# Output projection and second MLP matrix of a two-layer trunk: products of 512 columns instead of 256, and the weight block in the outer loop

## The chip, the core and the metric

One core of one Trainium2 chip runs the whole program in one launch. The metric is the device time of an execution in microseconds (us), lower is better. The kernel before takes 1643.44 us (median of 3 runs, 1642.19 to 1646.79).

## What is computed

Two layers over 256 latent tokens and 256 context tokens of width 1024, all in float32. In the last layer the context only gives keys and values, so what lies behind the mixer runs over 512 tokens in the first layer and over 256 in the last. The part that matters here:

```python
def merge_out(gates, ys, wb, bb, wo):
    ...                                   # merged: (tokens, 1024)
    return merged @ wo                    # wo: (1024, 1024)

def sq_relu_ffn(h, w1, w2):
    a = jax.nn.relu(h @ w1)               # (tokens, 4096)
    return (a * a) @ w2                   # w2: (4096, 1024)

x = layer_norm(DEEPNORM_ALPHA * x + g1 * y, ln_g[l, 0], ln_b[l, 0])
x = layer_norm(DEEPNORM_ALPHA * x + g2 * sq_relu_ffn(x * (1.0 + sc2) + sh2, w_ff1[l], w_ff2[l]),
               ln_g[l, 1], ln_b[l, 1])
```

## The kernel before, in words

**Arithmetic.** Every float32 operand is split into a high part (rounded to the matmul's float32 format) and a low part (what is left). A product is three matmuls: high times high, high times low, low times high (`mm3`, L424). The program's names show it: `whi` and `wlo` are the two parts of a weight unit, `mg` the merged branches (in pairs of tiles, high and low), `a` the squared activations of the MLP.

**Weight units.** All weights come in units of 128 partitions x 1024 values (512 KB). For each unit SyncE issues a transfer into one of three `raw` buffers (`w_load`), ScalarE copies it to one of three `whi` buffers (`w_hi`), VectorE subtracts to one of three `wlo` buffers and frees the raw one (`w_lo`). A unit's `whi` and `wlo` come free when TensorE has read them for the last time. Units come in the order of `weight_order` (L614), the order in which the matmuls use them.

**The two products of this case.** In the output projection (`out_proj`, tile name `wo`) and the second MLP matrix (`ff2`, tile name `f`) the tokens are the stationary operand: one matmul has 128 tokens as weights and streams 256 columns of a weight unit. A unit holds 512 rows (4 blocks k of 128) of 256 output columns. Outer loop: four column blocks nb of 256; both units of the block are fetched (`weights`, L599); inner loop: the tiles of 128 tokens; per tile 8 k times 3 matmuls into one PSUM bank, then the next tile. So in a token tile the 24 matmuls run over all 8 k before the next tile begins, and the two units of a block are held until the last tile has used them. The MLP's 4096 rows come in four quarters (qd 0 to 3) of 1024, with stretches of the first MLP matrix (`ff1`, tile name `mm`) between them; the quarters are summed in `yacc` on VectorE. In layer 0, `out_proj` and the last quarter run over two pairs of token tiles (s = 0, 1), the other quarters over all four; in layer 1 there is one pair.

**What follows a product.** `residual` (L1413) multiplies the PSUM result by the gate row, adds the scaled input, and takes the norm's statistics (BN_STATS), each on VectorE over 256 columns; in a last quarter the input was added ahead (`ffn_residual`). `norm_tile` waits for the four statistics of a token tile and normalises it (`r` is such a tile; `st` its statistics); TensorE transposes it (`uT`), ScalarE and VectorE make the next product's operand `u`.

**Order of the work.** A list scheduler at build time (`Sched.run`) replays costs and priorities and writes one fixed order per engine; at run time each engine goes through its own list in order and waits on semaphores. The modulation sums of layer 1 (`sums`, from transfers named `araw`) are woven into layer 0 on VectorE and ScalarE; `araw` has two buffers. In the last layer four of a stage's eight units serve each token tile in turn (`blocks`, L607: the first two column blocks for both tiles, then the other two for tile 0 alone, then for tile 1); two of those units are held in other buffers (`wh`, `wl`).

Of the kernel before, what the change touches and what calls it, by code (L numbers as in the profile page):

```python
# [54 lines left out]
def unit_table():  # L55

    names = []
    for m in range(76):
        if not (M_DV <= m < M_DV + 4 or M_NV <= m < M_NV + 4):
            names.append(("in", m))  # L60
    for br in ("dv", "nv"):
        names += [(br, s, h) for s in range(2) for h in range(2)]
    names += [("br", i, mp) for i in range(4) for mp in range(4)]
    names += [("wo", nb, h) for nb in range(4) for h in range(2)]
    names += [("f1", m) for m in range(32)]
    names += [("f2", qd, nb, h) for qd in range(4) for nb in range(4) for h in range(2)]
    return {n: i for i, n in enumerate(names)}
# [237 lines left out]
class Kernel(Sched):  # L305
# [126 lines left out]
    def gemm(self, out, pairs, cost):  # L432
# [3 lines left out]
        for i in range(0, n, step):  # L436
            calls, r = [], []
            for j in range(i, min(n, i + step)):
                a, b = pairs[j]
                calls += self.mm3(out, a, b, j == 0, j == n - 1)  # L440
                r += [a[0], a[1], b[0], b[1]]
            yield self.mm(calls, [out], r, (cost + 2) * len(calls))

# [145 lines left out]
    def weight(self, l, *name):  # L589
# [6 lines left out]
        kn = 128 if name[0] in ("in", "f1") else 256  # L596
        return Weight(w, kn)

    def weights(self, l, name):  # L599
        w = []  # L600
        for h in range(2):
            x = yield from self.weight(l, *name, h)
            w.append(x)
        return w

    @staticmethod
    def blocks(l):  # L607

        both = (0, 1)
        if l < DEPTH - 1:  # L610
            return [(nb, both) for nb in range(4)]
        return [(0, both), (1, both), (2, (0,)), (3, (0,)), (2, (1,)), (3, (1,))]

    def weight_order(self):  # L614
        o = []
        for l in range(DEPTH):
# [37 lines left out]
            for s in range(S):  # L654
                for nb in range(4):
                    a("wo", nb, 0)
                    a("wo", nb, 1)
            f1 = lambda m0, m1: [a("f1", m) for m in range(m0, m1)]
            f2 = lambda qd: [a("f2", qd, nb, h) for nb in range(4) for h in range(2)]
# [730 lines left out]
    def normalise(self, r, stv, gb=None):  # L1390

        nc = self.nc
        st4 = stv[:, 0:24].re("p (c n) -> p c n", n=6)
# [19 lines left out]
    def residual(self, l, j, s, t, cols, ps, r, x, gB, stv, part):  # L1413

        nc = self.nc
        if part is None:
            yield self.tt(r, ps, gB, ALU.mult)
            self.release(ps)
            yield self.stt(r, x, ALPHA, r, ALU.mult, ALU.add)
        else:  # L1420
            f = yield self.s("tmp", F32, "yf")
            yield self.tt(f[:, 0:256], ps, gB, ALU.mult)
            self.release(ps)
            yield self.wait("pre", l, t, cols)
            yield self.tt(r, f[:, 0:256], r, ALU.add)
            self.release(f)
        o = stv[:, cols * 6:cols * 6 + 6]
        yield self.dve(335, lambda: nc.vector.bn_stats(out=o.ap, in_=r.ap), [o], [r])
        self.signal("res", l, j, t, cols)
# [20 lines left out]
    def norm_tile(self, l, j, t, r, stv):  # L1450
# [5 lines left out]
        for nb in range(4):  # L1456
            yield self.wait("res", l, j, t, nb)
# [3 lines left out]
        yield from self.normalise(r, stv, gb)  # L1461
# [23 lines left out]
    def out_proj(self, l, s, merged):  # L1485
# [14 lines left out]
        ws = {}  # L1500
        for nb, which in self.blocks(l):
            if nb not in ws:
                ws[nb] = yield from self.weights(l, ("wo", nb))
            w = ws[nb]
            c = slice((nb % 2) * 256, (nb % 2) * 256 + 256)
            for i in which:
                ps = yield self.alloc("ps", "main", name="wo")
                tk = slice(s * 256 + i * 128, s * 256 + i * 128 + 128)
                yield from self.gemm(ps[:, 0:256], [(self.cut(merged[k], (slice(None), tk)), w[k // 4](k % 4))
                                                    for k in range(KD)], 107)  # L1510
                self.spawn(self.residual(l, 0, s, 2 * s + i, nb, ps[:, 0:256], rs[i][nb // 2][:, c],
                                         xs[i][nb // 2][:, c], gB[nb // 2][:, c], sts[i], None), 2)
            if which[-1] == 1:
                for x in w:
                    self.release(*x.views())
        self.spawn(self.free_rows(("gB", l, 0, s), [("res", l, 0, 2 * s + i, nb) for i in range(2) for nb in range(4)]), 50)
# [53 lines left out]
    def ff2_evac(self, l, qd, t, nb, ps, y):  # L1570
# [5 lines left out]
        if qd == 2:  # L1576
            self.spawn(self.ffn_residual(l, t, nb, y), 55)

    def ffn_residual(self, l, t, nb, y):
# [3 lines left out]
        c = slice((nb % 2) * 256, (nb % 2) * 256 + 256)  # L1583
        yield self.tt(y, y, gB[nb // 2][:, c], ALU.mult)
        yield self.stt(y, x[nb // 2][:, c], ALPHA, y, ALU.mult, ALU.add)
        self.signal("pre", l, t, nb)

    def ff2(self, l, qd, tiles, last):
# [14 lines left out]
        ws = {}  # L1603
        for nb, which in self.blocks(l) if last else [(nb, range(len(tiles))) for nb in range(4)]:
            if nb not in ws:
                ws[nb] = yield from self.weights(l, ("f2", qd, nb))
            w = ws[nb]
            c = slice((nb % 2) * 256, (nb % 2) * 256 + 256)
            for t in [tiles[i] for i in which]:
                ps = yield self.alloc("ps", "main", name="f2")  # L1610
                tk = slice(t * 128, t * 128 + 128)
                yield from self.gemm(ps[:, 0:256], [(self.cut(a2[k], (slice(None), tk)), w[k // 4](k % 4))
                                                    for k in range(8)], 107)
# [259 lines left out]
```

## Time and profile before

| | |
|---|---|
| median of 3 runs | 1643.44 us (1642.19 to 1646.79) |
| the profiled execution | 1644.06 us |
| its span, first to last instruction | 1642.3 us |
| granted TensorE clock, mean | 0.99 |
| TensorE busy | 1604.0 us, 98% of the span |
| VectorE busy | 1298.5 us, 79% |
| ScalarE busy | 884.6 us, 54% |
| DMA, mean | 155 GB/s |

A row of the profile gives an engine, its line, the operation, the output and inputs by the program's names, the shape and the count; times in a row are us unless marked ns. All matmuls are issued on L423, transposes on L449. `PE` is TensorE, `PEld` its loading of the stationary operand, `DVE` VectorE, `ACT` ScalarE, `SP` SyncE (which issues all transfers). The duration that is printed for a matmul is a model of its end; the distance between starts is measured.

### The profile page before, as it was taken

The page shows a single profiled execution, that of the slowest core. Times are in us where ns is not written, and L with a number is a line of the kernel's source. Part 1 is how long each engine was busy: PE and PEld are TensorE (multiplying, and loading weights), DVE is VectorE, ACT ScalarE, POOL GpSimd, SP SyncE. Part 2 cuts the span into 40 slices and gives each one's busy share as a digit, 9 for nine tenths or more (in the row PEclk, how much of TensorE's full clock was granted, in tenths as well). Part 3 has the DMA queues.
Part 4 walks back from the last instruction along what each step waited for, and adds up shares of the span by engine and source line. Part 5 has one row for each costly group of instructions (what it writes and reads, how often), then busy time and mean ns, then how long its engine had stood idle before and what let it go on. Part 6 is the DMA issues. An engine that isn't in the chain of part 4 may idle for free.

```text
span 1642.3 us, 26846 instructions
## 1 busy us (share of the span) xinstructions
PE 1604.0 (98%) x10568; PEld 1451.5 (88%) x10568; DVE 1298.5 (79%) x2285; ACT 884.6 (54%) x1444; POOL 11.0 (1%) x51
## 2 busy tenths in 40 slices
PE   7999999999999999999999999998999999989997
PEld 4888888887888889889898889998999999989997
DVE  3899999699999448875877866999999796774566
ACT  3475484556655344642524324665677675466553
POOL 0000000000000000000000000000000000000000
PEclk9999999999999999999999999999999999999999
DMA  9322322553552345455656634634353445636563
GB/s 356 114 81 77 97 74 90 186 189 126 176 172 95 109 148 182 158 192 161 208 175 207 219 98 134 192 115 141 114 163 125 146 133 185 226 129 183 187 218 119
DMA packets 81299, 254.55 MB, mean 155 GB/s; under 512 B 9092, under 2 KB 14980, under 8 KB 81172
## 3 DMA queue, kind: packets, MB, share of 16 engines
q1 hardware_dynamic: 81172, 252.84, 47.5%
q8 instruction: 82, 1.34, 0.3%
q14 instruction: 45, 0.37, 0.1%
HBM read 250.67 MB, written 2.13 MB: 154 GB/s over the span
## 4 chain that ended last, share of the span: by engine, by line
PE 89%; DMA 5%; DVE 4%; ACT 2%; issue 1%; SPq 0%; POOLq 0%; POOL 0%; DVEq 0%; ACTq 0%
PE mm L423 50%; PE f L423 13%; PE br L423 8%; PE v L423 5%; PE wo L423 4%; PE o L423 2%; DMA araw<-in_w_ada 2%; PE S L423 2%; PE PT L449 1%; DVE wlo L376 1%; DMA a<-in_w_ada 1%; DVE sums L403 1%; ACT whi L369 1%; PE ada L423 1%; SPq L414 0%
## 5 line engine op out<-in xcount | busy, mean ns | idle before, releaser
L423 PE MATMUL mm<-u,whi 128*128 128x512 f32 (+1 forms) x3168 | 791.8, 341 | 2.4 <-ACT u L369 1.6
L369 ACT ACTIVATE whi<-raw 128x1024 fp32r<-128x1024 f32 x335 | 354.4, 1059 | 481.5 <-PE mm L423 236.9
L423 PEld LDWEIGHTS mm<-u,whi 128*128 128x128 f32 x3168 | 548.3, 192 | 67.1 <-ACT u L369 2.5
L376 DVE TENSOR_TENSOR wlo<-raw,whi 128x1024 fp32r<-128x1024 f32 x335 | 408.7, 1222 | 198.4 <-ACT whi L369 195.2
L423 PE MATMUL mm<-u,wlo 128*128 128x512 f32 (+1 forms) x1584 | 536.3, 339 | 0.8 <-DVE wlo L376 0.8
L423 PEld LDWEIGHTS mm<-u,wlo 128*128 128x128 f32 x1584 | 303.5, 192 | 32.6 <-DVE wlo L376 1.0
L423 PE MATMUL f<-whi,a 128*128 128x256 f32 x1504 | 276.6, 285 | 0.5 <-ACT a L369 0.2
L423 PEld LDWEIGHTS f<-whi,a 128*128 128x128 f32 x1504 | 237.0, 193 | 3.6 <-issue 2.5
L423 PE MATMUL f<-wlo,a 128*128 128x256 f32 x752 | 213.8, 284 | 2.6 <-DVE wlo L376 2.6
L403 DVE SCALAR_TENSOR_TENSOR sums<-araw,cs,sums 128x512 f32<-128x512 f32 x280 | 194.8, 744 | 25.3 <-DMA araw<-in_w_ada 25.0
L423 PEld LDWEIGHTS f<-wlo,a 128*128 128x128 f32 x752 | 145.0, 193 | 3.4 <-DVE wlo L376 3.2
L403 DVE SCALAR_TENSOR_TENSOR conf<-glu,sm,conf 128x512 f32<-128x512 f32 (+1 forms) x240 | 137.9, 612 | 1.0
L423 PE MATMUL v<-whi,u 128*128 128x256 f32 x512 | 96.7, 283 | 0.3 <-DVE pt L376 0.3
L423 PEld LDWEIGHTS v<-whi,u 128*128 128x128 f32 x512 | 81.6, 191 | 1.5 <-PE S L423 0.7
L423 PE MATMUL v<-wlo,u 128*128 128x256 f32 x256 | 72.4, 283 | 0.0
L369 ACT ACTIVATE P<-S,st 128x512 f32<-128x512 f32 (+1 forms) x96 | 58.4, 612 | 24.0 <-DVE st L1150 23.5
L423 PE MATMUL wo<-whi,mg 128*128 128x256 f32 x352 | 67.3, 289 | 3.1 <-ACT mg L369 2.6
L423 PEld LDWEIGHTS wo<-whi,mg 128*128 128x128 f32 x352 | 56.7, 196 | 4.1 <-ACT mg L369 3.0
L1150 DVE TENSOR_REDUCE st<-S 128x1 f32<-128x512 f32 (+1 forms) x96 | 55.5, 589 | 1.5 <-PE S L423 1.3
L369 ACT ACTIVATE qk<-ra 64x512 fp32r<-64x512 f32 (+1 forms) x74 | 42.8, 578 | 20.2 <-DVE ra L376 18.8
L423 PE MATMUL o<-pt,v 128*128 128x256 f32 x360 | 47.9, 285 | 2.7 <-ACT pt L369 1.4
L423 PE MATMUL wo<-wlo,mg 128*128 128x256 f32 x176 | 50.4, 286 | 0.0
(194 smaller groups left out, 1910.9 us busy)
## 6 DMA issues: line engine op xcount, KB each, us to landing
raw<-in_W SPq DMA_DIRECT2D x344, 512.0 KB
araw<-in_w_ada SPq DMA_DIRECT2D x80, 512.0 KB
a<-in_w_ada SPq DMA_DIRECT2D x32, 256.0 KB
bt<-in_rpb SPq DMA_DIRECT2D x32, 128.0 KB
row<-g SPq DMA_DIRECT2D x12, 256.0 KB
x<-in_x_t SPq DMA_DIRECT2D x8, 256.0 KB
row<-in_ln_g SPq DMA_DIRECT2D x8, 256.0 KB
row<-in_ln_b SPq DMA_DIRECT2D x8, 256.0 KB
```

Source lines behind the costliest of these rows:

```text
L369: lambda: nc.scalar.activation(out=out.ap, in_=in_.ap, func=func, **kw),
L376: return self._op(eng, cost, lambda: e.tensor_tensor(out=out.ap, in0=x.ap, in1=y.ap, op=op), [out], [x, y])
L403: return self._op("DVE", cost, lambda: nc.vector.scalar_tensor_tensor(out=out.ap, in0=x.ap, scalar=a(s), in1=y.ap, op0=op0, op1=op1), [out ...
L423: nc.tensor.matmul(out=out, lhsT=x, rhs=y, start=start, stop=stop, **kw)
L449: nc.tensor.transpose(o.ap, i.ap, ident.ap)
L1150: yield self.dve(68 + 1.04 * nk, lambda: nc.vector.tensor_reduce(out=mx.ap, in_=S.ap, axis=AX.X, op=ALU.max, negate=True), [mx], [S])
```

## The change

The weight units of `wo` and `f2` are cut the other way: 256 rows (2 blocks k) of 512 columns. There are two column blocks nb of 512 and four units q in each. A new helper `wide` takes one unit at a time in the outer loop and goes over the token tiles in the inner one; each tile has its own PSUM bank of 512 columns, open over the four units. What follows a product works on 512 columns. In the last layer the second block goes through its four units for tile 0, and then once more for tile 1, there in two pieces of 256 columns (`parts`), and tile 1's statistics stay at 256 (`grain`). The held units are the first two of that block.

```diff
-    names += [("wo", nb, h) for nb in range(4) for h in range(2)]
+    names += [("wo", nb, q) for nb in range(2) for q in range(4)]
...
+    def wide(self, l, name, nb, which, tiles, a, ws, done):
+        parts = self.parts(l, nb, which, tiles)
+        for c0, cw in parts:
+            ps = {}
+            for q in range(4):
+                if len(ws) <= q:
+                    w = yield from self.weight(l, *name, q)
+                    ws.append(w)
+                w = ws[q]
+                for i in which:
+                    if not q:
+                        ps[i] = yield self.alloc("ps", "main", name=name[0])
+                    tk = slice(i * 128, i * 128 + 128)
+                    yield from self.gemm(ps[i][:, 0:cw], [(self.cut(a[2 * q + k], (slice(None), tk)), w(k, slice(c0, c0 + cw)))
+                                                          for k in range(2)], 0.4167 * cw, q == 0, q == 3)
+                    if q == 3:
+                        done(i, nb * 512 + c0, cw, ps[i])
+                if which[-1] == tiles[-1] and (c0, cw) == parts[-1]:
+                    self.release(*w.views())
+    def parts(l, nb, which, tiles):
+        if l == DEPTH - 1 and nb == 1 and len(tiles) == 2 and which == (tiles[1],):
+            return [(0, 256), (256, 256)]
+        return [(0, 512)]
+    def grain(l, i):
+        return 256 if l == DEPTH - 1 and i == 1 else 512
...
-            return [(nb, both) for nb in range(4)]
-        return [(0, both), (1, both), (2, (0,)), (3, (0,)), (2, (1,)), (3, (1,))]
+            return [(0, (0, 1)), (1, (0, 1))]
+        return [(0, (0, 1)), (1, (0,)), (1, (1,))]
...
-        for nb, which in self.blocks(l):
-            if nb not in ws:
-                ws[nb] = yield from self.weights(l, ("wo", nb))
-            ...
-            for i in which:
-                ps = yield self.alloc("ps", "main", name="wo")
-                ...
-                yield from self.gemm(ps[:, 0:256], [(self.cut(merged[k], (slice(None), tk)), w[k // 4](k % 4))
-                                                    for k in range(KD)], 107)
+        ws = [], []
         for nb, which in self.blocks(l):
+            yield from self.wide(l, ("wo", nb), nb, tuple(2 * s + i for i in which), (2 * s, 2 * s + 1), merged, ws[nb], done)
...
-                          if l == DEPTH - 1 and (n[:2] == ("wo", 2) or n[:3] == ("f2", 3, 2))}
+                          if l == DEPTH - 1 and (n[:2] == ("wo", 1) and n[2] < 2 or n[:3] == ("f2", 3, 1) and n[3] < 2)}
...
-                W[l, i] = a_unit(f["w_o"][l][name[2] * 512:name[2] * 512 + 512], name[1] * 256, 4, 256)
+                W[l, i] = a_unit(f["w_o"][l][name[2] * 256:name[2] * 256 + 256], name[1] * 512, 2, 512)
```

`ff2` changes in the same way, and `residual`, `ff2_evac` and `ffn_residual` take 512 columns at a time.

What it moves, at two places. **TensorE at the start of layer 0's output projection.** The first matmul of the stage, then the matmuls that first read the last two merged tiles (`mg_5889` and `mg_5890` are the high and low part of the seventh, `mg_5934` and `mg_5935` of the eighth). Before:

```order
L423 MATMUL wo_5944<-whi_5822,mg_5523 128x256
...
L423 MATMUL wo_5944<-whi_5860,mg_5889 128x256
L423 MATMUL wo_5944<-wlo_5864,mg_5889 128x256
L423 MATMUL wo_5944<-whi_5860,mg_5890 128x256
L423 MATMUL wo_5944<-whi_5860,mg_5934 128x256
L423 MATMUL wo_5944<-wlo_5864,mg_5934 128x256
```

And now:

```order
L423 MATMUL wo_5944<-whi_5822,mg_5523 128x512
...
L423 MATMUL wo_5952<-whi_5898,mg_5814 128x512
L423 MATMUL wo_5944<-whi_5959,mg_5889 128x512
L423 MATMUL wo_5944<-wlo_5976,mg_5889 128x512
L423 MATMUL wo_5944<-whi_5959,mg_5890 128x512
L423 MATMUL wo_5944<-whi_5959,mg_5934 128x512
```

Before, 21 matmuls of 256 columns, all of the first token tile, stand ahead of the first use of the eighth merged tile; now 39 matmuls of 512 columns on two token tiles do, and the weights there are the stage's fourth unit.

**VectorE where layer 0's output projection passes to the first MLP matrix.** The normalisation of the last token tile (`r_6213` before, `r_6103` now: the half that VectorE does) and the first modulation sums, which wait for `araw`. Before:

```order
L383 TENSOR_SCALAR st_6214<-st_6214 128x1
L376 TENSOR_TENSOR x1_5661<-x1_5661,row_5578 128x512
L383 TENSOR_SCALAR r_6213<-r_6213,st_6214 128x512
L376 TENSOR_TENSOR x1_5663<-r_5939,row_5581 128x512
L383 TENSOR_SCALAR sums_6598<-araw_6605,cs_83 128x512
L383 TENSOR_SCALAR uf_6664<-uT_6657,G01_5900,B01_5901 128x256
```

And now:

```order
L1421 BN_AGGR st_6105<-st_6105 128x2
L383 TENSOR_SCALAR sums_6354<-araw_6361,cs_83 128x512
L383 TENSOR_SCALAR st_6105<-st_6105 128x1
L383 TENSOR_SCALAR sums_6356<-araw_6361,cs_83 128x512
L383 TENSOR_SCALAR sums_6358<-araw_6379,cs_83 128x512
L383 TENSOR_SCALAR st_6105<-st_6105 128x1
L383 TENSOR_SCALAR sums_6360<-araw_6379,cs_83 128x512
L383 TENSOR_SCALAR r_6103<-r_6103,st_6105 128x512
```

The last tile's normalisation stood ahead of the first sum; now it stands behind four sums, which need two `araw` transfers.

## Rows read from the trace of the kernel before

**Rows 1.** The page: the span; busy time of each engine with its share of the span; the chain of work that ended last, by engine.

```profile
span 1642.3 us, 26846 instructions
PE 1604.0 (98%) x10568; PEld 1451.5 (88%) x10568; DVE 1298.5 (79%) x2285; ACT 884.6 (54%) x1444; POOL 11.0 (1%) x51
...
PE 89%; DMA 5%; DVE 4%; ACT 2%; issue 1%; SPq 0%; POOLq 0%; POOL 0%; DVEq 0%; ACTq 0%
```

**Rows 2.** Groups of TensorE instructions by shape, whole span: line, engine, operation, output and inputs, stationary shape, streamed shape, count, then busy us and mean ns of one (modelled ends), then idle time before them.

```profile
L423 PE MATMUL f<-whi,a 128*128 128x256 f32 x1504 | 276.6, 285 | 0.5 <-ACT a L369 0.2 <-DVE a L376 0.2
...
L423 PE MATMUL f<-wlo,a 128*128 128x256 f32 x752 | 213.8, 284 | 2.6 <-DVE wlo L376 2.6
...
L423 PE MATMUL wo<-whi,mg 128*128 128x256 f32 x352 | 67.3, 289 | 3.1 <-ACT mg L369 2.6 <-DVE mg L376 0.5
L423 PE MATMUL wo<-wlo,mg 128*128 128x256 f32 x176 | 50.4, 286 | 0.0
```

**Rows 3.** The chain of work that ended last: start, length, work, count of matmuls. `mm` of layer 0 streams 512 columns, `f` and `mm` of layer 1 stream 256.

```profile
779.06 43.55 PE mm L423 x192
...
1477.74 23.04 PE f L423 x192
1500.78 23.04 PE mm L423 x192
```

**Rows 4.** TensorE in order of time at the start of layer 0's output projection: start, length, instruction, count; in brackets the idle time before it and what ended it.

```profile
615.83 0.28 PE L423 MATMUL wo<-whi,mg 128*128 128x256 f32 x1
617.82 0.39 PE L423 MATMUL wo<-whi,mg 128*128 128x256 f32 x1 [1.71 <-ACT mg L369]
...
618.55 0.51 PE L423 MATMUL wo<-whi,mg 128*128 128x256 f32 x2 [0.22 <-DVE mg L376]
```

**Rows 5.** Three stretches: from:to, length, TensorE busy (instructions), granted clock as a share of 2.4 GHz, DMA share, GB/s.

```profile
617.80:622.40 4.60, 4.35 (x22) 0.64 0.81 294
676.50:687.40 10.90, 9.86 (x38) 0.69 0.15 48
929.70:933.10 3.40, 3.36 (x15) 0.50 0.56 170
```

**Rows 6.** The chain in the third quarter of layer 0's second MLP matrix: start, length, work.

```profile
921.86 5.91 DMA araw<-in_w_ada
...
928.47 1.23 DVE wlo L376
...
929.74 18.86 PE f L423 x143
```

**Rows 7.** TensorE in order of time, waits in the first quarter, at the start of the last quarter of layer 0, and at the start of layer 1's output projection.

```profile
766.37 0.38 PE L423 MATMUL f<-wlo,a 128*128 128x256 f32 x1 [0.46 <-DVE wlo L376]
...
1002.33 0.39 PE L423 MATMUL f<-whi,a 128*128 128x256 f32 x1 [0.23 <-ACT a L369]
1003.06 0.50 PE L423 MATMUL f<-whi,a 128*128 128x256 f32 x2 [0.23 <-DVE a L376]
...
1416.54 0.38 PE L423 MATMUL wo<-whi,mg 128*128 128x256 f32 x1 [0.28 <-DVE mg L376]
1417.78 0.38 PE L423 MATMUL wo<-whi,mg 128*128 128x256 f32 x1 [0.86 <-ACT mg L369]
```

**Rows 8.** Waits of VectorE from 729 to 1003 us: who waited for whom, us in total, times, longest.

```profile
DVE sums L403 <- DMA araw<-in_w_ada: 22.5, 11, 4.6
```

**Rows 9.** The chain where layer 0's output projection passes to the first MLP matrix.

```profile
667.28 6.97 DMA araw<-in_w_ada
...
674.26 1.95 ACT sums L369 x3
```

**Rows 10.** TensorE in order of time at the same place.

```profile
674.23 1.47 PE L449 MATMUL uT<-ident,r 128*128 128x128 f32 x12
676.57 0.84 PE L423 MATMUL mm<-u,whi 128*128 128x256 f32 x2 [0.87 <-ACT u L369]
```

**Rows 11.** Stretches from layer 0's last quarter into layer 1: from:to, length, busy us (instructions) of PE, PEld, DVE, ACT, POOL, then granted clock, DMA share, GB/s.

```profile
1003.00:1049.00 46.00, 45.94 (x384) 45.95 (x385) 39.25 (x80) 24.21 (x32) 1.65 (x3) 1.00 0.54 171
1049.00:1080.00 31.00, 31.00 (x241) 30.02 (x240) 29.09 (x55) 22.54 (x39) 1.24 (x9) 1.00 0.68 209
1080.00:1110.00 30.00, 30.00 (x217) 28.37 (x216) 29.11 (x67) 19.34 (x39) 0.00 (x0) 1.00 0.28 85
1110.00:1135.00 25.00, 20.64 (x155) 19.62 (x154) 24.30 (x51) 15.64 (x23) 0.00 (x0) 0.92 0.47 152
```

**Rows 12.** Groups of VectorE and ScalarE instructions by shape, as in rows 2.

```profile
L376 DVE TENSOR_TENSOR wlo<-raw,whi 128x1024 fp32r<-128x1024 f32 x335 | 408.7, 1222 | 198.4 <-ACT whi L369 195.2 <-PE PT L449 1.0
...
L376 DVE TENSOR_TENSOR yf<-f,row 128x256 f32<-128x256 f32 x24 | 10.0, 417 | 2.9 <-PE f L423 2.9
...
L376 DVE TENSOR_TENSOR x<-r,row 128x512 f32<-128x512 f32 x12 | 8.2, 684 | 0.0
...
L369 ACT ACTIVATE whi<-raw 128x1024 fp32r<-128x1024 f32 x335 | 354.4, 1059 | 481.5 <-PE mm L423 236.9 <-PE f L423 131.6 <-issue 43.1
```

**Rows 13.** The chain in the last stage: a weight transfer.

```profile
1617.09 5.04 DMA raw<-in_W
```

**Rows 14.** Waits of ScalarE from 1500 to 1524 us, in the first MLP matrix of layer 1.

```profile
ACT whi L369 <- PE mm L423: 6.0, 8, 1.4
```

More of the change, by code (lines that the diff above doesn't have):

```diff
@@ L430, in mm3, with gemm @@
         return [(out.ap, x.ap, y.ap, first and j == 0, last and j == 2, {}) for j, (x, y) in enumerate(o)]
-    def gemm(self, out, pairs, cost):
+    def gemm(self, out, pairs, cost, first=True, last=True):
         n = len(pairs)
@@ L595, in weight @@
         w = yield self.wait("w", i)
-        kn = 128 if name[0] in ("in", "f1") else 256
+        kn = {"in": 128, "f1": 128, "wo": 512, "f2": 512}.get(name[0], 256)
         return Weight(w, kn)
[L599 to L604, printed above, removed]
     @staticmethod
     def blocks(l):
-        both = (0, 1)
         if l < DEPTH - 1:
-            return [(nb, both) for nb in range(4)]
-        return [(0, both), (1, both), (2, (0,)), (3, (0,)), (2, (1,)), (3, (1,))]
+            return [(0, (0, 1)), (1, (0, 1))]
+        return [(0, (0, 1)), (1, (0,)), (1, (1,))]
     def weight_order(self):
@@ L654, in weight_order @@
             for s in range(S):
-                for nb in range(4):
-                    a("wo", nb, 0)
-                    a("wo", nb, 1)
+                for nb in range(2):
+                    for q in range(4):
+                        a("wo", nb, q)
             f1 = lambda m0, m1: [a("f1", m) for m in range(m0, m1)]
-            f2 = lambda qd: [a("f2", qd, nb, h) for nb in range(4) for h in range(2)]
+            f2 = lambda qd: [a("f2", qd, nb, q) for nb in range(2) for q in range(4)]
             f1(0, 8)
@@ L1411, in normalise, with residual @@
         self.release(stv)
-    def residual(self, l, j, s, t, cols, ps, r, x, gB, stv, part):
+    def residual(self, l, j, s, t, c0, cw, ps, r, x, gB, stv, ahead):
         nc = self.nc
-        if part is None:
-            yield self.tt(r, ps, gB, ALU.mult)
+        if not ahead:
+            yield self.tt(r, ps[:, 0:cw], gB, ALU.mult)
             self.release(ps)
@@ L1455, in norm_tile @@
             gb = g, b
-        for nb in range(4):
-            yield self.wait("res", l, j, t, nb)
+        ns = 1024 // self.grain(l, t)
+        for n in range(ns):
+            yield self.wait("res", l, j, t, n)
         if gb:
@@ L1460, in norm_tile @@
                 self.spawn(self.store_out(t, c, r[c]), 5)
-        yield from self.normalise(r, stv, gb)
+        yield from self.normalise(r, stv, ns, gb)
         self.signal("z", l, j, t)
@@ L1602, in ff2, with done @@
             self.spawn(self.after_ffn_norm(l, s, [yacc[t] for t in tiles], [xs[t] for t in tiles]), 2)
[L1603 to L1613, printed above, removed]
-                y = yacc[t][nb // 2][:, c]
-                if last:
-                    self.spawn(self.residual(l, 1, s, t, nb, ps[:, 0:256], y, xs[t][nb // 2][:, c],
-                                             gB[nb // 2][:, c], sts[t], y), 2)
-                else:
-                    self.spawn(self.ff2_evac(l, qd, t, nb, ps[:, 0:256], y), 9)
-            if which[-1] == len(tiles) - 1:
-                for x in w:
-                    self.release(*x.views())
+        def done(t, c0, cw, ps):
+            h, c = c0 // 512, slice(c0 % 512, c0 % 512 + cw)
+            if last:
+                self.spawn(self.residual(l, 1, s, t, c0, cw, ps, yacc[t][h][:, c], xs[t][h][:, c], gB[h][:, c], sts[t], True), 2)
+            else:
+                self.spawn(self.ff2_evac(l, qd, t, h, ps, yacc[t][h]), 9)
+        ws = [], []
+        for nb, which in self.blocks(l) if last else [(nb, range(len(tiles))) for nb in range(2)]:
+            yield from self.wide(l, ("f2", qd, nb), nb, tuple(tiles[i] for i in which), tuple(tiles), a2, ws[nb], done)
         if not last or tiles[-1] == len(yacc) - 1:
```

57 lines of the change are left out of this document (28 added, 29 removed).

## Prediction, written before the changed kernel was run

> **What bounds the kernel now.** I read the page first: TensorE is busy for 98% of the span and makes up 89% of the chain of work that ended last [rows 1]. So what TensorE saves should come off the span, unless another engine or a transfer then ends later than it; the rest of the reading looks for places of that kind. Next the groups by shape, to count what changes: the two products are made of matmuls that stream 256 columns, 1504 + 752 for `f` and 352 + 176 for `wo` [rows 2], and with those on the held units, by the loops, 30 passes of a token tile (20 in layer 0, 10 in layer 1) of 4 blocks x 24 = 2880. Then the chain, for what one costs in a stream: 192 with 256 columns take 23.04 us, 192 with 512 columns 43.55 us [rows 3], so 0.1200 and 0.2268 us from start to start. I took these and not the modelled durations of a matmul, which overlap. Last, the waits of TensorE in the changed stages and just behind them [rows 4 to 7, 9 to 11].
>
> **Part 1, the matmuls: 18.4 us less.** One matmul of 512 columns takes the place of two of 256 and saves 2 x 0.1200 - 0.2268 = 0.0132 us. By the loops 30 passes x 48 = 1440 would be wide; the two passes over tile 1 of layer 1 that keep 256 columns in their second block turn 48 of them back into 96 narrow ones, so 1392 pairs are saved: 1392 x 0.0132 = 18.4 us. It is all on the path, since TensorE runs without a gap through most of these stages [rows 3]. The rule that speaks against this is in the Trainium skill, page "TensorE: Matmul & The Clock Gate", section "Back-to-back issue gap": a warm matmul takes its columns at 2.4 GHz plus a fixed 2.5 ns or so. By that page a pair would save 2.5 ns and this part would be an estimated 3.5 us. The trace does not agree: at 0.1200 and 0.2268 us the fixed share is 13.3 ns [rows 3].
>
> **Part 2, waits that lose their cause: 10.8 us less.** Two things move. A token tile now reads the last of its eight k tiles late in the stage, and a weight unit is given back as soon as all tiles have used it.
> - *Start of layer 0's output projection.* After 21 matmuls TensorE waits for the eighth merged tile, 615.95 to 617.82, and for its low part until 618.55 [rows 4]; its clock then falls for a while, a mean of 0.64 between 617.8 and 622.4 [rows 5]. The gaps are 1.87 + 0.39 us, and some 17 matmuls at 1.2 GHz cost 0.213 instead of 0.120 us, 1.6: 3.9 us in all. Now 39 matmuls of 512 columns stand ahead of that read, 8.8 us instead of 2.5, so the tile is there 3 us before it is needed. The fourth unit's weights are needed at the same point; their buffer comes free after 2.7 us and the copy and the subtraction take 1.06 and 1.22 us [rows 12], which fits.
> - *Third quarter of layer 0.* A block's second unit needs the buffer of the previous block's first unit, which the fourth tile reads until 10.1 us into the block, and is needed itself after 13.0: 2.9 us for 1.06 + 1.22. VectorE was held by an `araw` transfer, the subtraction began at 928.47 and TensorE at 929.74 [rows 6], 2.4 us late, then 15 matmuls at a clock of 0.50 [rows 5], 1.4: 3.8 us. Now a unit takes 24 x 0.2268 = 5.44 us, and one that takes over a buffer has two units' time, 10.9 us. That leaves 8.6, and VectorE's longest wait for `araw` is 4.6 [rows 8]. The same cause gives 0.7 at 766.37 [rows 7].
> - *Layer 0's last quarter and layer 1's output projection* wait for their last k tile: 1.0 and 1.9 us [rows 7]. I take the first, and of the second only 1.0, since the seventh and eighth units there pass through a transfer (5.04 us in [rows 13]), a copy and a subtraction, and now come within about half a us of being late. In the last stage some 0.4 of the same kind goes.
> Sum 3.9 + 3.8 + 0.7 + 1.0 + 1.0 + 0.4 = 10.8. Bounds: nothing and 11.7 (all of layer 1's too).
>
> **Part 3, what it adds: 3.7 us.**
> - *From layer 0's output projection to the MLP.* The normalisation of the last token tile now stands on VectorE behind four sums that need two `araw` transfers; the first of these landed at 674.2 after 6.97 us, and ScalarE's three sums ended at 676.2 [rows 9]. TensorE, done with what it had at 675.7, began again at 676.57 [rows 10] and ran at a mean clock of 0.69 until 687.4 [rows 5], while `u` came from ScalarE tile by tile. For it: the last unit but one is given back earlier, so the weight transfer that stands ahead of `araw` in SyncE's queue, and with it `araw`, can go some 2 us earlier against the end of the stage; the second `araw` now also stands ahead of the next weight transfer. Against it: the chain behind it is longer by a normalisation, a transpose, two operations for `u`, about 2.5 us, and by three wider operations of the last block. I take 1.5 more, between 2 less and 5 more.
> - *VectorE at the start of layer 1.* It is busy 82.5 of the 86 us from 1049 to 1135, and TensorE waits there for it, busy 20.6 of the last 25 [rows 11]. What VectorE has left when the last quarter ends therefore counts. The last block's three operations per tile cost 3 x 0.684 instead of 3 x 0.417 [rows 12], 0.8 more behind the end, though over the stage VectorE has less to do (two of 256 cost 0.15 more than one of 512). I take 0.8, between 0 and 2.6, all that the matmuls save in that quarter (192 x 0.0132).
> - *The end.* Tile 0's last block is wider, its normalisation ends later, and one of its operations (0.7) comes between those of tile 1: 0.4.
> - *Waits not seen before.* In the four-tile stages all four PSUM banks are open through a block. A tile's bank is wanted again 3 x 1.36 = 4.1 us after its end, its evacuation takes 0.68, and VectorE can be held for 4.6: up to 1.2 us late at each of four changes of block or stage. I take 1.0, between 0 and 5.
>
> The copies and subtractions for weights stay as many and as long, one set for each unit, and lie beside the matmuls as before; transfers keep number, size and queue.
>
> **Sum.** 18.4 + 10.8 - 3.7 = 25.5 us less than the profiled execution's 1644.06 us, which has a span of 1642.3 and stands 0.6 above the median of 1643.44; from that median, **1618 us**.
>
> **Rivals.**
> - *The waits only change places*: part 1 holds, part 2 gives nothing. For it: VectorE is near its limit in several stages, and each order is fixed by a scheduler that does not see real transfer times. Against: the new slacks of 3 to 8 us. 1643.4 - 18.4 + 3.7 = 1628.7.
> - *A wide matmul on weights costs as much as two narrow ones*: 0.2268 was measured with tokens streamed and weights stationary, here it is the other way round. Against: with 256 columns both ways cost 0.1200 [rows 3], `f` with tokens stationary and `mm` with weights. Then 1643.4 - 10.8 + 3.7 = 1636.3. By the Trainium skill's gap (same page and section) it would be an estimated 1632.8, 3.5 less.
> - *Slower: the loop of three raw buffers becomes the bound.* In the two-tile stages a unit now lasts 12 x 0.2268 = 2.72 us instead of 2.88. A raw buffer goes round in transfer + 1.06 + 1.22 + 0.1 us and must do so in three units, 8.16. It decides from a landing time of 5.8 us on. At the 7.0 that `araw` took in [rows 9] the round is 9.4, a unit 3.12, and 72 such units (16 + 16 in layer 0, 8 + 32 in layer 1) cost 29 us: 1618 + 29 = 1647; at 7.2, 1652. For it: transfers land late where several overlap, as there. Against: a weight transfer landed after 5.04 us [rows 13], and in layer 1, at 2.88 us per unit, ScalarE's copies wait for TensorE to give back a buffer and not for a transfer [rows 14].
> That the change does not do what it says is excluded: the order shows 512 columns and the unit in the outer loop.
>
> **How the numbers follow.** Forecast 0.81, waits that change places 0.10, no gain per matmul 0.06, slower 0.03. Low end: all of part 2 (11.7), 2 saved after the output projection, no other cost, and 2 more if VectorE's lighter load shortens its wait in layer 1: 1643.4 - 18.4 - 11.7 - 4 = 1609. High end: half of part 2 and all upper bounds of part 3 (5 + 2.6 + 0.4 + 5): 1643.4 - 18.4 - 5.4 + 13 = 1632, which takes in the first rival. About 0.3% (5 us) is what a measurement of this kernel can tell from no change; all cases but the slower one, and a little at the edge of the second rival, are faster by more: 0.95, 0.02 and 0.03.
>
> **What would show it.** In the profile after, 192 `f` in a row take 43.5 us; TensorE has no gap in the first 9 us of layer 0's output projection, which shrinks from 52 to about 45.5 us; the subtraction for a weight no longer ends a wait of TensorE in layer 0's quarters; the wait before `mm` after the output projection is longer; VectorE is still above 90% busy early in layer 1. It is wrong if 192 `f` take over 45 us, or if ScalarE's copies wait for `raw` transfers in the two-tile stages.

## The result and the profile after

The changed kernel takes **1621.79 us** (median of 4 runs, 1615.51 to 1623.89) against 1642.82 for the kernel before beside it; the ratio is 0.9863 with a 95% interval of 0.9829 to 0.9896 (the two medians alone give 0.9872). Run again unaltered (`repeat` below) it takes 1619.00 (4 runs, 1618.35 to 1621.80) against 1642.01, ratio 0.9864, 0.9850 to 0.9877. The forecast was 1618.0, the range 1609 to 1632. As a gain, where 25.5 us were forecast: 21.0 and 23.0 by the medians, 22.5 (17.1 to 28.1) and 22.3 (20.2 to 24.6) by the ratios.

The page of the changed kernel's first profile, the lines that answer [rows 1]:

```profile
span 1613.4 us, 23929 instructions
PE 1579.5 (98%) x9176; PEld 1373.1 (85%) x9176; DVE 1283.7 (80%) x2173; ACT 881.4 (55%) x1432; POOL 13.2 (1%) x51
...
PE 93%; DVE 3%; DMA 2%; ACT 2%; issue 1%; SPq 0%; POOLq 0%; POOL 0%; DVEq 0%; ACTq 0%
```

TensorE's share of the chain went from 89 to 93%, that of DMA from 5 to 2%. Its matmuls are 1392 fewer (10568 - 9176), as counted by the loops. The chain answers [rows 3]: start, length, work, count.

```profile
612.07 31.28 PE wo L423 x138
...
720.98 36.72 PE f L423 x162
...
767.09 43.52 PE mm L423 x192
...
810.61 36.72 PE f L423 x162
...
1453.00 21.79 PE f L423 x96
```

An unbroken piece of `wo` or `f` with 512 columns has the same pace as `mm`: 36.72 / 162 = 0.2267 us, 192 in 43.5 us. The 96 that do the work of 192 in layer 1 take 21.79 instead of 23.04. There is no break in the first 31 us of layer 0's output projection.

This table is worked out from the starts of TensorE's matmuls, in us: for each product the time from the start of its first to the start of its last matmul, for a passage from the last start of one to the first of the next; its last row runs from the last start to the end of the span. Each column is one profiled execution. (`narrow`, `pace112` are runs of the next section.)

| stretch | before | after | repeat | narrow | pace112 |
|---|---|---|---|---|---|
| output projection, layer 0 | 51.61 | 44.74 | 44.74 | 47.23 | 44.74 |
| passage to the MLP's `f` | 64.59 | 64.17 | 64.33 | 64.43 | 62.07 |
| first quarter | 49.13 | 45.89 | 45.89 | 48.43 | 43.29* |
| second quarter | 48.42 | 45.89 | 45.89 | 48.43 | 43.29* |
| third quarter | 52.11 | 45.89 | 48.48 | 48.43 | 43.29* |
| last quarter, both pairs | 48.63 | 44.72 | 44.71 | 47.23 | 44.72 |
| to layer 1's output projection | 365.65 | 366.72 | 367.24 | 366.74 | 366.51 |
| output projection, layer 1 | 24.78 | 22.87 | 22.86 | 23.52 | 22.86 |
| passage to `f` | 39.09 | 39.69 | 40.02 | 39.52 | 39.59 |
| each of three quarters, layer 1 | 22.92 | 21.56 | 21.56 | 22.92 | 21.56 |
| last stage | 23.53 | 22.51 | 22.05 | 22.92 | 22.54 |
| from its last matmul to the end | 8.69 | 9.36 | 9.35 | 9.36 | 9.36 |

*The 16 `ada` matmuls and 4 transposes inside these quarters (2.6 us) stand behind them there.

The first profile was taken in the quickest execution of its four, the second in the slowest. Between them, 1615.51 and 1621.80, lie three differences, beside smaller ones that cancel: 3.18 us before the output projection (first `wo` at 611.90 and 615.08), 2.59 in the third quarter and 0.52 behind the last. The first is not the change's: TensorE's 3212 instructions up to there are the same in the same order in both kernels, and in the profiles of this document the first `wo` starts anywhere from 611.90 to 616.94. The second is not noise. The chain of the second profile, third quarter:

```profile
897.95 7.81 DMA araw<-in_w_ada
...
915.64 6.49 DMA araw<-in_w_ada
...
928.55 1.32 DVE sums L403 x2
...
941.47 1.34 DVE sums L403 x2
...
942.85 1.90 PE ada L423 x6
944.75 1.59 PE f L423 x6
```

The transfers that made VectorE late in [rows 6] still do; what waits for it now is not a weight but the product `ada` of the finished sums, which stands in this quarter in TensorE's order. In the first profile the same 16 matmuls waited for nothing. That is the exception: with the sums at this pace the third quarter, 45.89 without such a wait, takes 47.11 in `only_f2`, 48.14 in `early_k` and 48.32 in `raw2` below.

### The profile page after: what moved, and what is told of

The parts are those of the page before. It is cut to its first block, busy times and chain, and to the rows that moved or that the text cites. A ratio compares the mean times of both kernels' runs of the same rounds, so it can differ in the third digit from the quotient of the medians.

```text
span 1613.4 us, 23929 instructions
## 1 busy us (share of the span) xinstructions
PE 1579.5 (98%) x9176; PEld 1373.1 (85%) x9176; DVE 1283.7 (80%) x2173; ACT 881.4 (55%) x1432; POOL 13.2 (1%) x51
## 4 chain that ended last, share of the span: by engine, by line
PE 93%; DVE 3%; DMA 2%; ACT 2%; issue 1%; SPq 0%; POOLq 0%; POOL 0%; DVEq 0%; ACTq 0%
PE mm L423 52%; PE f L423 15%; PE br L423 8%; PE v L423 6%; PE wo L423 3%; PE o L423 2%; PE S L423 2%; PE PT L483 1%; PE ada L423 1%; DMA araw<-in_w_ada 1%; DVE wlo L376 1%; ACT whi L369 1%; DMA raw<-in_W 1%; PE uT L483 0%; PE ms L423 0%
## 5 line engine op out<-in xcount | busy, mean ns | idle before, releaser
L423 PE MATMUL f<-whi,a 128*128 128x512 f32 (+1 forms) x760 | 236.4, 388 | 0.0
L423 PEld LDWEIGHTS f<-whi,a 128*128 128x128 f32 x760 | 142.4, 188 | 31.2 <-issue 2.5
L423 PE MATMUL f<-wlo,a 128*128 128x512 f32 (+1 forms) x380 | 147.4, 388 | 0.2 <-DVE wlo L376 0.2
L423 PEld LDWEIGHTS f<-wlo,a 128*128 128x128 f32 x380 | 71.4, 188 | 14.7 <-DVE wlo L376 0.6
L423 PE MATMUL wo<-whi,mg 128*128 128x512 f32 (+1 forms) x184 | 56.3, 382 | 0.0
L369 ACT ACTIVATE qk<-ra 64x512 fp32r<-64x512 f32 (+1 forms) x74 | 42.8, 578 | 20.2 <-DVE ra L376 18.8
L423 PEld LDWEIGHTS v<-wlo,u 128*128 128x128 f32 x256 | 49.0, 191 | 0.8
L423 PEld LDWEIGHTS o<-pt,v 128*128 128x128 f32 x360 | 45.7, 192 | 3.8 <-ACT pt L369 1.6
```

Source lines behind the costliest of these rows:

```text
L369: lambda: nc.scalar.activation(out=out.ap, in_=in_.ap, func=func, **kw),
L423: nc.tensor.matmul(out=out, lhsT=x, rhs=y, start=start, stop=stop, **kw)
```

## Experiments

**repeat: the changed kernel again.** No edit.

> The changed kernel once more, unaltered, because its profiled execution (1615.5 us) lies 5.5 to 8.4 us below the three others. Theory A: executions differ in when transfers land, and the slower ones hold waits of TensorE that the profiled one lacks; then the median stays at 1622 (1619 to 1624), and a second profile that falls near 1622 shows 5 to 8 us more of TensorE's idle time, most of it in one or two stages that wait for araw or for a weight unit. Theory B: an execution under the profiler is itself quicker; then the second profile is near 1615 again while the others stay near 1622. Theory C: the first profile was a stray; the second is within 2 us of the median and its stages differ from the first's by less than 0.5 us each, spread evenly.

Median 1619.00; its profile is of the slowest execution and names the two places above, so theory A holds for the profile, with half of the difference at the start, where no stage of the change lies. B and C fall: the profiled run was not the quickest.

**narrow: the new order with matmuls of 256 columns.**

```diff
+        if halves:
+            return [(out.ap[:, c:c + 256], x.ap, y.ap[:, c:c + 256], first and j == 0 and c == 0, last and j == 2 and c == 256, {})
+                    for j, (x, y) in enumerate(o) for c in (0, 256)]
```

> Keeps the new order (unit outer, token tile inner, units of 256 rows x 512 columns) but issues each product of 512 columns as two matmuls of 256 into the two halves of the same PSUM bank: 1392 matmuls more. It takes back part 1 alone. My theory (the width itself saves 0.0132 us per pair): 18.4 us slower than the changed kernel, 1640 if that has 1622; the stage of layer 0's output projection 45.0 + 192 x 0.0132 = 47.5 us, a four-tile quarter 46.1 + 2.5 = 48.6, 192 f in a row 23.04. Rival (a wide matmul costs as much as two narrow ones, and all was won by the order): within 2 us of the changed kernel, stages unchanged. What is left against the kernel before is then the order's own share: by the prediction 10.8 - 3.7 = 7 us.

1634.02 (5 runs, 1633.48 to 1636.05), 15.0 us slower than `repeat`; against before 0.9953 (0.9940 to 0.9967), 8.0 us, which is the share of all that is not the width of a matmul: the order, the cut of the units and the wider operations behind a product, which stay. VectorE, ScalarE and GpSimd have the same instructions in the same order here as in the changed kernel, so nothing else was altered. The rival falls. By the table an output projection of layer 0 costs 2.49 more, a quarter 2.54, layer 1's quarters 1.36 each. What is missing of 18.4 is, in the two profiles, the third quarter (equal to `repeat`'s, which had its wait) and waits in layer 1 that slower matmuls cover.

**narrow_pace112: the same on a base without that wait.** `narrow` with the edit of `pace112` below.

> The changed kernel with sums four units later, each wide product again issued as two of 256 columns. It repeats the test of part 1 on a base whose profile shows no wait in the third quarter; on the other base the difference was 15.0 us and not 18.4, and the two profiles there differ by a wait of 2.6 us in that quarter. Theory A (1392 pairs at 0.0132 us, less only small waits in layer 1's output projection and at the end that the slower matmuls cover): 16.5 to 18.4 us slower than the run with sums four units later, 1633 to 1635. Theory B (the width is worth less than 0.0132 us a pair, 0.0108 by 15.0 / 1392): 15 us slower, 1631.5, with the four-tile quarters less than 2.3 us longer.

1633.56 (1632.73 to 1634.64), 17.1 us slower than `pace112`, and 16.8 from the first `wo` to the end in the two profiles: theory A. The chains of `pace112`, then of this run, show one quarter as one piece:

```profile
723.92 43.52 PE f L423 x192
```

```profile
724.31 46.07 PE f L423 x384
```

The same work in the same order: 2.55 us for 192 pairs, 0.0133 a pair, with two matmuls in a row on the same stationary operand, which is loaded for each of them (10568 loads for 10568 matmuls).

**only_f2 and only_wo: one product changed at a time.** In the first `("wo", nb, h)` units, `blocks` and the loop over tiles are those of before, in the second those of `f2`.

> Only the second MLP matrix gets wide units and the new order; the output projection stays as it was before. My theory, from the stages of the two profiles: the four quarters of layer 0 give 15.5 us, those of layer 1 4.8, the start of layer 1 and the end take back 1.6 to 2.2; 18 us less than before, 1625. The first 9 us of layer 0's output projection keep the 3.9 us of waits and low clock. Rival (the changes share VectorE and the transfers, and part of the MLP's gain hangs on the output projection's new order): the quarters still give 15 us, but 3 us or more come back in the passage from the output projection to the MLP or in layer 1.

> Only the output projection gets wide units and the new order; the second MLP matrix stays as before. My theory: layer 0's output projection 6.8 us less, layer 1's 1.9 less, the passage to the MLP within 1 us of before: 9 us less, 1634; the third quarter of layer 0 keeps its wait of 2.4 us and the low clock behind it, 3.8 in all. With the run in which only the second MLP matrix is changed it should add up to the whole within 2 us. Rival (as there): the gains do not add up, the two alone giving 4 us or more above or below the whole.

`only_f2`: 1628.16 (1624.67 to 1629.48), 13.9 us less than before; `only_wo`: 1633.03 (1631.78 to 1634.28), 9.0 less. Together 22.8, and the whole in the same comparison 23.0: they add up, the rival falls. My 18 for `only_f2` was too much, since I took it from the quickest execution; in its own profile, again the quickest, the third quarter takes 47.11, since `ada` waits there too. Its output projection keeps 51.60, as expected; `only_wo`'s third quarter is 49.91, a wait of 1.39 for `wlo` and not 2.4.

**early_k: the last merged tiles read early again.**

```diff
+EARLY = (0, 3, 1, 2)
...
+        Q = EARLY if (l, name[0]) == (0, "wo") else (0, 1, 2, 3)
-                    yield from self.gemm(ps[i][:, 0:cw], [(self.cut(a[2 * q + k], (slice(None), tk)), ...
+                    yield from self.gemm(ps[i][:, 0:cw], [(self.cut(a[2 * Q[q] + k], (slice(None), tk)), ...
```

> The changed kernel, but in layer 0's output projection the four units of a block come in the order 0, 3, 1, 2, so that the last two merged tiles are read again after 12 wide matmuls, 2.7 us into the stage, as before (2.5 us). My theory (part 2, first term: the late read is what won there): the wait of TensorE for the merged tile and its low part is back at 615 to 619 us, 1 to 2.3 us, with a low granted clock behind it, and the stage takes 47 to 49 us instead of 45.0; 2 to 4 us slower than the changed kernel. Rival (the stage was won by the weights alone, since a unit that takes over a buffer now has two units' time): no wait for a merged tile, the stage within 0.7 us of 45.0.

The stage takes 46.13, 1.39 more; the total, 1622.97 (1619.64 to 1624.76), ratio 0.9876 (0.9862 to 0.9889), can't be told from the changed kernel's. The waits for both parts of the tile are back (for the low one it is the load of the stationary operand that waits, 0.43 us), but with no fall of the clock, so the stage stays below the 47 to 49 us that I had said. TensorE in order of time, in brackets the idle time before it, and two stretches with the granted clock behind the busy times:

```profile
619.63 0.50 PE L424 MATMUL wo<-whi,mg 128*128 128x512 f32 x1 [0.82 <-ACT mg L370]
...
620.36 0.73 PE L424 MATMUL wo<-whi,mg 128*128 128x512 f32 x2
```

```profile
615.00:620.00 5.00, 4.18 (x19) 3.11 (x17) 2.90 (x4) 2.69 (x4) 0.00 (x0) 1.00 0.25 84
620.00:625.00 5.00, 5.00 (x22) 3.87 (x21) 2.75 (x3) 1.59 (x2) 0.00 (x0) 1.00 0.99 325
```

I had counted to the seventh tile. The eighth is read after 15 matmuls, 3.40 us, where before it was read after 21 narrow ones, 2.52: 0.88 later, and 1.87 - 0.88 = 0.99 is the gap measured (0.98 from start to start). In both kernels the tile's high part is first used 4.38 us after the stage's first matmul and its low part 5.11 us after it (617.82 and 618.55 - 613.44; 619.63 and 620.36 - 615.25), so the tile comes when it did, and the read's place sets the wait. The slow starts around the two waits make up the 1.39 us of the stage. That is a part of the 4.4 us that the stage gained: the rest is mainly the 0.88 and the low clock, which this run did not bring back. With waits of this length the clock stayed at 1.00, where [rows 5] had 0.64.

**pace112 and pace116: the modulation sums four and eight units later.**

```diff
-ADA_PACE = 108
+ADA_PACE = 112
```

> The changed kernel with the modulation sums of layer 1 (and their araw transfers) begun four weight units later, so that the last token tile's normalisation in the passage from layer 0's output projection to the MLP stands ahead of the first sums. Theory A (what is left of the waits hangs on araw transfers that VectorE waits for in its fixed order): the passage shrinks from 64.2 to 61 to 63 us, and the wait in the third quarter that differs between executions (none in one, 2.6 us in the other, for the sums) goes or stays short; 2 to 5 us faster, 1614 to 1617. Theory B (the passage is bound by its own chain of normalisation, transposes and u; the transfer is hidden beside it): the passage within 0.5 us of 64.2, the total within 2 us of the changed kernel's, unless sums that come later meet other work; in that case the start of layer 1 is longer than 367.

> As the run with sums four units later, but eight. Theory A: as there, 2 to 5 us faster than the changed kernel, passage 61 to 63 us. Theory B: passage near 64.2, total within 2 us. If the sums are now late for layer 1, TensorE waits before layer 1's first products: the stretch from the last quarter to layer 1's output projection is then longer than 367 us by more than 1.

1616.46 (5 runs, 1614.51 to 1617.94), ratio 0.9835 (0.9822 to 0.9849), and 1616.28 (1614.69 to 1617.33), ratio 0.9836 (0.9823 to 0.9850): both beat both kernels, the changed one by 2.5 to 5.5 us against its two medians. The passage falls to 62.07 in both, the third quarter has no wait in either, and the start of layer 1 is no longer than in the changed kernel: theory A. Only 2.1 us of the passage hung on `araw`; what is left of it ends, in `pace112` too, with the chain from the normalisation to `u`.

**before_pace112: the same edit in the kernel before.**

> The kernel before (256 columns, token tile outer), with the modulation sums of layer 1 begun four weight units later. Theory A (the wait in the third quarter and part of the passage were the araw transfers' doing and could be had without the change): the third quarter, less the 16 ada matmuls and 4 transposes that move out of it (2.6 us), falls from 52.1 to 45.8 to 46.5, that is 3 to 3.7 us of it are won; the passage falls by 2 us; 1636 to 1638 in all. Then 4 to 6 us of the change's gain are not its own, and against this base it gives some 20 us and not 25. Theory B (the old order of the units runs short of buffers wherever VectorE is held, so the wait moves with the sums): the quarter's wait appears in another place, and the total is within 2 us of before.

1641.59 (11 runs), ratio 0.9993 (0.9981 to 1.0005): no gain, theory B, though the two quickest of the 11, 1637.04 and 1637.97, lie where theory A had them and have no profile. The chain in the third quarter, then TensorE there:

```profile
921.66 5.35 DMA araw<-in_w_ada
...
927.70 1.23 DVE wlo L376
...
928.97 21.06 PE f L423 x161
```

```profile
928.97 0.38 PE L423 MATMUL f<-wlo,a 128*128 128x256 f32 x1 [2.59 <-DVE wlo L376]
```

Another `araw` transfer of the same sums now holds VectorE at the same point, and the subtraction is late as in [rows 6]. In `pace112`, with the sums at the same pace, TensorE waits for nothing in that quarter; but VectorE waits less there (1.6 us), so the better comparison is `narrow_pace112`, which has the same pace of the sums and the same width of the matmuls as this run. VectorE's waits for `araw` in the third quarter (us in total, times, longest), first in this run, then there, and TensorE's quarter there:

```profile
DVE sums L403 <- DMA araw<-in_w_ada: 3.6, 2, 1.8
```

```profile
DVE sums L403 <- DMA araw<-in_w_ada: 7.4, 3, 3.1
```

```profile
908.74 46.07 PE f L423 x384
```

VectorE is held longer and TensorE does not stop. In `before_pace112` the passage falls, to 61.56, and of these 3.0 us 2.3 are given back in the quarters and the stretches between them.

**raw2: two raw buffers in the changed kernel.**

```diff
-            "raw": Resource(big, "raw", [128, 1024], 3),
+            "raw": Resource(big, "raw", [128, 1024], 2),
```

> The changed kernel with two raw buffers in place of three, for the rival in which this loop becomes the bound. With two, it decides from a landing of 2 x 2.72 - 1.06 - 1.22 - 0.1 = 3.06 us on, in two-tile stages, where transfers in layer 1's quarters land 2.9 to 3.1 us after their issue, by the profile. (The build gives some other instructions a new order too.) Theory A (the loop works as the rival says and stands at its edge now): quarters of layer 1 21.6 to 22.5 us instead of 21.6, losses where transfers overlap with araw or others, 3 to 20 us slower in all; ScalarE's copies there wait for transfers and no longer for TensorE. Theory B (transfers queue behind one another, a second one in flight does not shorten the wait, and the loop needs three): quarters of layer 1 25 us and longer, 40 us or more slower in all.

1669.35 (5 runs, 1667.76 to 1677.46), ratio 1.0155 (1.0135 to 1.0174): 50 us slower than `repeat`, of the size of theory B, but not by its mechanism alone. The profile is of the slowest execution. There the first two quarters of layer 1 take 24.5 and 24.4 us, between the two theories, and the third 27.87; 8 to 10 us each go in layer 0's output projection (52.44) and last quarter (53.84), in layer 1's output projection (32.52) and in the last stage (31.99). ScalarE's copies of weights in the MLP of layer 1, in `raw2` from 1500 to 1640 us and in the changed kernel's first profile from 1453 to 1591; behind the bar busy us, mean ns, then idle time before them and what ended it:

```profile
L369 ACT ACTIVATE whi<-raw 128x1024 fp32r<-128x1024 f32 x44 | 46.6, 1058 | 66.1 <-DMA raw<-in_W 62.3 <-DVE yacc L376 2.3 <-DVE wlo L376 1.3
```

```profile
L369 ACT ACTIVATE whi<-raw 128x1024 fp32r<-128x1024 f32 x48 | 50.9, 1060 | 52.6 <-PE f L423 35.1 <-PE mm L423 17.5
```

With two buffers the loop is the bound there, with three it is not. Single transfers in the chain of `raw2` landed after 3.38, 5.05 and 4.09 us, where the formula, to cost nothing, allowed 3.06. Since the build also changes the order of other instructions, it is not shown that all of the 50 us are the loop's.

## Why the prediction came out right, step by step

**Part 1 (18.4): right.** 17.1 us measured on a base without waits, 15.0 on the other, and 0.0133 us a pair where I had 0.0132. The second rival is ruled out, and with it the 3.5 us. The Trainium skill's page "TensorE: Matmul & The Clock Gate", section "Back-to-back issue gap", gives its fixed 2.5 ns for an isolated matmul, which the prediction did not say; in this kernel's stream the runs show 13.3 ns (2 x 0.1200 - 0.2267 us).

**Part 2 (10.8): right, a little small.** `narrow` has the width of before, so the table shows the order's terms, each from one profile of either kernel: start of the output projection 4.4 (I had 3.9), first quarter 0.7 (0.7), third quarter 3.7 (3.8), last quarter 1.4 (1.0), layer 1's output projection 1.3 (1.0), last stage 0.6 (0.4): 12.0. The causes were tried for two. `early_k` moves the read of the merged tile forward, and its waits come back as long as the read's place says; the low clock behind them did not, so that share of the 4.4 is argued. `before_pace112` and `narrow_pace112` show that a late VectorE costs TensorE 2.6 us in the old order and none in the new one. The others were not tried by themselves.

The two places in the changed kernel, where [rows 5] had clocks of 0.64 and 0.50: the start of the output projection, then the whole third quarter, in its first profile. TensorE is busy throughout at a clock of 1.00.

```profile
612.00:617.00 5.00, 5.00 (x24) 4.15 (x23) 3.21 (x4) 2.96 (x4) 0.00 (x0) 1.00 0.33 113
617.00:622.40 5.40, 5.40 (x26) 4.46 (x25) 3.45 (x3) 2.31 (x3) 0.00 (x0) 1.00 0.94 308
...
900.00:946.00 46.00, 46.00 (x214) 36.78 (x213) 40.55 (x58) 10.25 (x11) 0.00 (x0) 1.00 0.56 183
```

**Part 3 (3.7): two of its terms wrong, two too small, and one wait not foreseen.**

*The passage (+1.5) was 0.3 to 0.4 shorter instead.* The chain there, answering [rows 9]:

```profile
658.18 7.70 DMA araw<-in_w_ada
...
665.91 0.49 DVE sums L383
...
666.91 0.46 DVE r L383
667.37 0.61 DVE x L376
...
673.82 1.22 PE mm L423 x4
```

The transfer does go earlier against the last `wo` matmul (1.5 us behind it, 2.2 before), by 0.7 us where I had said some 2, and takes 0.7 longer, 7.70 against 6.97; the normalisation (`r`) does stand behind the sums, and from there VectorE's chain to `u` sets the pace until 673.8. But `u` now comes in short steps: the longest gap of TensorE is 1.28 us (before 1.02), and the clock between 671 and 682 us 0.84, where [rows 5] had 0.69 over a stretch of the same length:

```profile
671.00:682.00 11.00, 10.04 (x66) 9.43 (x67) 9.97 (x19) 9.59 (x18) 0.00 (x0) 0.84 0.08 26
```

I had priced the longer chain and not that the clock would be low for a shorter time. That this balances the chain is argued, not tried by itself; what the transfer is worth was tried, 2.1 us (`pace112`).

*The start of layer 1 (+0.8) cost 0.6 to 1.6, for a reason I did not give.* I took VectorE's load as the cause. It is as loaded as before (29.1 of 30 us, as in [rows 11]):

```profile
1058.00:1088.00 30.00, 30.00 (x217) 28.38 (x216) 29.11 (x66) 19.47 (x38) 0.00 (x0) 1.00 0.28 93
1088.00:1113.00 25.00, 21.13 (x151) 20.02 (x150) 24.29 (x52) 16.23 (x23) 0.00 (x0) 0.88 0.42 142
```

But TensorE's three waits behind it are as long as before (1.57, 1.59 and 1.43 to 1.77 us of gap; before 1.57, 1.59 and 1.78), and two of the three are ended by ScalarE (its `pt` and `osq`), not by VectorE as I had read. What is new is a gap of 0.71 at the first product of layer 1, which waits for the last tile's statistics:

```profile
1025.90 0.60 DVE st L1457
1026.51 0.59 DVE yf L376
1027.10 0.11 DVE st L1421
1027.21 0.29 DVE u L376
1027.50 0.07 DVE st L383
1027.57 4.45 PE mm L423 x35
```

It is there in `narrow` too (366.74), though its last quarter gives VectorE 2.5 us more, and in `only_f2` (366.85), and not in `only_wo` (364.49), whose last quarter is the old one. So it is the wider operations at the quarter's end or the order around them, not a backlog; the runs do not part the two.

`only_wo` lies 1.2 us below before although TensorE has the same 2746 instructions there in the same order. The difference is the clock behind the three waits. From 3.0 us behind the last of them, first before, then in `only_wo` (busy times, then granted clock, as in [rows 11]):

```profile
1135.30:1138.30 3.00, 3.00 (x17) 3.00 (x17) 2.68 (x8) 0.48 (x3) 0.13 (x2) 0.57 0.00 0
```

```profile
1126.30:1129.30 3.00, 3.00 (x27) 3.00 (x27) 2.77 (x9) 1.66 (x4) 0.13 (x2) 1.00 0.00 0
```

By execution, 8 to 22 `mm` matmuls run there at the lower of the two clocks, 1.2 GHz, 0.213 us from start to start instead of 0.120. With 0.093 us taken off for each, the start of layer 1 takes 1.3 to 1.5 us more than before in all eight profiles of this document that have the new cut of `f2` and three `raw` buffers, and the same as before in the two that have the old cut. So the term was 1.4 and not 0.8; 0.71 of it is the gap above, and the rest was not traced.

*The PSUM bank (+1.0) cost nothing*: in the first profile TensorE waits for nothing in the quarters of layer 0. *Not foreseen* was the wait of `ada` for the sums in the third quarter, 0 in one profile of the changed kernel and 2.6 in the other, and 0.6 to 0.9 in layer 1's passage to `f`, whose cause was not looked for. The end cost 0.67 (I had 0.4).

**The sum.** 18.4 + 12.0, less 1.3 of part 1 that covers waits elsewhere (18.4 - 17.1), 1.0 for the start of layer 1, 0.67 for the end, 0.6 for layer 1's passage and 0 to 2.6 for the sums, makes 24 to 27. Without what lies ahead of the first `wo`, the two profiles show 27.0 and 23.9 against the profile of before (28.55 - 1.54 and 22.26 + 1.64); the medians, with it, 21.0 and 23.0. That profile of before ran 1.2 and 2.1 us above the medians of before beside the two results, so the medians are the fairer measure, and by them the forecast of 25.5 was 2.5 to 4.5 too high; which stages hold that in the executions without a profile is not known. That it came so near is in part luck, errors that cancel. Better than I said were part 2 (1.2), the passage (1.8) and the PSUM bank (1.0); worse were the 1.3 of part 1, the start of layer 1 and the end (some 0.6 and 0.3), layer 1's passage (0.6 to 0.9) and the wait for the sums (up to 2.6), which was missing.

**The rivals.** That waits only change places was right for one of them: the third quarter's moved from `wlo` to `ada` in some executions, at two thirds of its size. The slower one did not come: in the first quarter of layer 1 (first profile, 1453 to 1475 us) ScalarE's copies wait, as in [rows 14], for TensorE and not for transfers:

```profile
ACT whi L369 <- PE f L423: 10.0, 8, 1.7
```

`raw2` shows that such a loop can become the bound and what it then costs: with one buffer less the two-tile stages lose.

## What to carry to other kernels

Measure the start-to-start time of a matmul at two widths in the kernel's own stream before changing widths: the fixed share per matmul times their number is the gain, and here, on the base without waits, it came out to within a tenth (17.1 of 18.4). An order in which every buffer has two units' time to refill doesn't remove an engine's lateness; here it kept it off the bound engine. Ask which product still stands where the late one is needed. Then move that: the edit of one number that did nothing for the old order gave the new one 2.5 to 5.5 us.

## What the runs showed of the hardware that I had not expected

The granted clock did not fall after every gap: 0.82 us of idle time in `early_k` left it at 1.00, and so did 1.2 in the third quarter of `only_wo` (1.00 from 922.2 to 926.0); 1.71 and 0.22 close together took it to 0.64 [rows 4, 5]. How long it stays low after the same gaps differs by execution: 8 matmuls in `only_wo`, 22 in `repeat`, 1.3 us apart. And the fixed 13.3 ns of a matmul stay when the next one uses the same stationary operand, loaded again (`narrow_pace112`: 0.1200 us for each of 384).
